# Weight blocks in another pool, X's updates with precedence, 1/rms transposed one product later

## The chip, the cores and the metric

The kernel runs on one core of one Trainium2 chip. The metric is the device time of one execution in microseconds (us), the median of several runs. A core has a matrix engine (TensorE, PE in the profile, with its weight loads as PEld), a vector engine (VectorE, DVE), an activation engine (ScalarE, ACT), a general engine (GpSimd, POOL) and SyncE (SP), which here only issues DMAs. Each works through its own instructions in order and waits on semaphores for the others. Work memory is SBUF (128 partitions); matmuls write to eight PSUM banks.

## What is computed

Two layers of a transformer with 512 tokens and width 1024 in float32: each layer is a half-step SwiGLU ffn, a mixer, and another half-step ffn, and every part is preceded by an RMS norm.

```python
def swiglu(h, w_in, w_out):
    a, b = jnp.split(h @ w_in, 2, axis=-1)
    return (jax.nn.silu(a) * b) @ w_out

for layer in range(DEPTH):                                             # 2
    g = norm_g[layer]
    x = x + 0.5 * swiglu(rmsnorm(x, g[0]), ffn_w_in[layer, 0], ffn_w_out[layer, 0])
    h = rmsnorm(x, g[1])
    x = x + (even_mixer(h, ...) if layer % 2 == 0 else odd_mixer(h, ...))
    x = x + 0.5 * swiglu(rmsnorm(x, g[2]), ffn_w_in[layer, 1], ffn_w_out[layer, 1])
return rmsnorm(x, final_norm_g)
```

The mixers are attention blocks (a gated linear attention beside a forgetting attention in the even one, an attention over the 256 best keys in the odd one). Of them only the end matters here: the output projection that is added to x.

## The kernel before

**Stages.** The program is one straight line of six stages and an end: ffn0, even, ffn1, ffn2, odd, ffn3, fin. x is kept transposed in SBUF as `X`, eight blocks of 128 features by 512 tokens.

**Precision.** Matmuls run on float32r operands. Each operand is split into a high part (`whi`, `th`, `hh`: a ScalarE copy) and a low part (`wlo`, `tl`, `hl`: a VectorE difference), and a product is three matmuls: high by high, high by low, low by high. `whi` and `wlo` have three buffers each.

**An ffn.** The 2816 hidden units are 11 pairs of 2 x 128. For each pair the first matrix product is done with seven block products instead of eight (Strassen-like). `Products` holds a pair's weight blocks `a11`, `a21` (in a `wraw` tile), `a22` and `a12`, and forms sums of them (`ws`) on VectorE in `side` (L131); `make` (L153) splits each into `whi` (L159, ScalarE) and `wlo` (L160, VectorE). The order of the products is p1, p5, p2, p6, p3, p7, p4, with p4 of a pair after p1 of the next. Each is 24 matmuls (L345). They use `th` and `tl`, combinations of the blocks of x, made by `combined` (L215) for each block as soon as X's block is final. For the first pair of an ffn `opening` (L347) runs p1, p5 and p2 first with three of the four block pairs of x (18 matmuls each) and then with the last one (6 each). The down products (eight blocks d of X, three groups of pairs; `mm3`, L195) follow in `sums` and `end` (L462 to L474): `down_end` scales the sum into `dn` (L428) and adds it to X (L429). In the last group `after(d)` then prepares the next stage's operands and the squares for the next norm.

**The norm.** The sum of squares becomes 1/rms for each token as a column, `Rc` (`rstd_cols`, L287; the rsqrt's last step is L276). `rstd_rows` (L303) transposes it to a row on all partitions with four matmuls (L307), and `rstd_tile` copies that to `R`. In pair 0 of every ffn `run` does this behind p3, and multiplies the first half of the pair's outputs by R and takes the SiLU; the later pairs use the same R.

**A mixer's end.** `out_units` (L533) loads `even_out` or `odd_out` in four `wraw` tiles, splits them (L84 and L88) and runs eight output products of 24 matmuls. `end(d)` adds the product to X (L548) and calls `after(d)`, which makes the next ffn's `th` and `tl` and adds the squares up on GpSimd (L259).

**Memory.** Pools are stacks from two ends of SBUF. From the left: small things, `wraw`, `wsp` (`whi` and `wlo`), and then, in a mixer, `mo` (operands, among them those of the output products), `mx` and `at` (scratch of attention); in an ffn `wx` (two `a22`, `a12` and `ws`, 4 KB each), `hp` and `ft`. From the right: `xp`. In an ffn it holds `th` and `tl` (four tiles of 7 KB each) and scratch of 8 KB; in a mixer `XGH` and `XGL`, eight tiles of 2 KB each. `open_in` (L1215) replaces `xp` shortly before the last output products, at which point a mixer has released `at` and `mx`. `xp` is opened with `reuse_waits="tile"`. `mo` is released only after the mixer's last instruction, and `wx` of the next ffn is allocated behind that.

**Order.** TensorE's instructions run in program order (`manual_schedule`). All others are put in order by a planner: it simulates the program and gives each engine, whenever it is free, the instruction with the lowest rank among those whose inputs are ready by its own clock; the rank is the place in the program. On the chip each engine then keeps to that order. SyncE's loads are in one queue in the same way.

Of the kernel before, what the change touches and what calls it, by code (L numbers as in the profile page):

```python
# [8 lines left out]
F32 = mybir.dt.float32  # L9
F32R = mybir.dt.float32r  # L10
U32 = mybir.dt.uint32
AF = mybir.ActivationFunctionType
# [3 lines left out]
S = 512  # L16
# [9 lines left out]
B11, T1, B21, B22, T2, T4, T3 = range(7)  # L26
# [72 lines left out]
class Products:  # L99
# [10 lines left out]
    def place(self, p, early):  # L110

        b = self.b
        w = self.blocks.setdefault(p, {})
        if early:
            raw = b.wraw.tile([128, 2048], F32, name="wraw")
            w["a11"], w["a21"] = raw[:, :1024], raw[:, 1024:]
            w["a22"] = b.wx.tile([128, 1024], F32, name="a22", bufs=2)
        else:
            w["a12"] = b.wx.tile([128, 1024], F32, name="a12", bufs=1)

    def fetch(self, p, n):
        c = ("a11", "a21", "a12", "a22").index(n) * 1024
# [8 lines left out]
    def side(self, p, q):  # L131

        w, v = self.blocks[p], self.b.nc.vector
        if q == "p1":
            return w["a11"]
        if q == "p2":
            return w["a12"]
        if q == "p4":
            return w["a22"]
        if q == "p5":  # L140
            w["s"] = self.b.wx.tile([128, 1024], F32, name="ws", bufs=1)
            v.tensor_add(w["s"], w["a21"], w["a22"])
            return w["s"]
        if q == "p6":
            v.tensor_sub(w["s"], w["s"], w["a11"])
            return w["s"]
        if q == "p3":
            v.tensor_sub(w["a12"], w["a12"], w["s"])
            return w["a12"]
        v.tensor_sub(w["a21"], w["a11"], w["a21"])  # L150
        return w["a21"]
# [12 lines left out]
class Builder:  # L164
# [160 lines left out]
    def ffn(self, n, after, first=None, lead=None):  # L325
# [5 lines left out]
        nc = self.nc  # L331
# [28 lines left out]
        def copy(name, bank, bufs):  # L360
            t = self.ft.tile([128, 2, HT], F32, name=name, bufs=bufs)
            nc.scalar.activation(t, bank.rearrange("p (f t) -> p f t", f=2), AF.Copy)
            return t

        def run(p, q, R):

            v = nc.vector
            three = lambda b: b.rearrange("p (f t) -> p f t", f=2)
            if q == "p1":
                if p:  # L370
                    d = st[p] = {"a": self.bank("ps")}
                    product(p, q, d["a"], B11, True)
                d = st[p]
                d["c1"] = copy("c1", d["a"], 1)
                return
            d = st[p]
            if q == "p5":
                if p:
                    d["b"] = self.bank("pt")
                    product(p, q, d["b"], T1, True)  # L380
                d["c5"] = copy("c5", d["b"], 1)
            elif q == "p2":
                if p:
                    d["c"] = self.bank("s")
                    product(p, q, d["c"], B21, True)
                d["t"] = self.ft.tile([128, 2, 2, HT], F32, name="ta", bufs=2)
                v.tensor_add(d["t"][:, :, 0], d["c1"], three(d["c"]))
            elif q == "p6":
                product(p, q, d["a"], T2, False)
                d["c2"] = copy("c2", d["a"], 1)  # L390
            elif q == "p3":
                product(p, q, d["b"], B22, False)
                if p == 0:
                    Rt.append(self.rstd_tile(d["rc"], "s"))
                v.tensor_add(d["t"][:, :, 1], d["c2"], three(d["b"]))
                t = d["t"].rearrange("p f h t -> p f (h t)")
                v.tensor_mul(t, t, R()[:, None, :].to_broadcast([128, 2, S]))
                self.table = "silu"
                nc.scalar.activation(t, t, AF.Silu)
            elif q == "p7":  # L400
                product(p, q, d["a"], T3, False)
                v.tensor_add(d["c5"], d["c5"], three(d["a"]))
            else:
                product(p, q, d["a"], T4, False)
                t = d["t"]
                v.tensor_mul(t[:, :, 1], t[:, :, 1], d["c5"])
                v.tensor_mul(t[:, :, 0], t[:, :, 0], three(d["a"]))
                h = [self.hp.tile([128, 2, S], F32R, name=x) for x in ("hh", "hl")]
                t = t.rearrange("p f h t -> p f (h t)")
                nc.scalar.activation(h[0], t, AF.Copy)  # L410
                v.tensor_sub(h[1], t, h[0].bitcast(F32))
                H[p] = h
                del st[p]
# [19 lines left out]
        R = lambda: Rt[0]  # L433
# [18 lines left out]
        for g, (a, b) in enumerate(GROUPS):  # L452
            last = b == NP
            seq = []
            for p in range(a + 1 if g else a, min(b + 1, NP)):
                ps = [(p, q) for q in Products.ORDER[:6]]
                if p:
                    ps.insert(1, (p - 1, "p4"))
                seq += ps
            round_(a, seq + [(NP - 1, "p4")] * last)  # L460
            banks = {}

            def begin(d):
                w = down_w(g, d)
                w.split(0)
                banks[d] = w, self.bank(tags[d % 5])

            def sums(d, pairs):
                down_mm(g, d, *banks[d], pairs)

            def end(d):
                down_end(d, banks.pop(d)[1], R())
                if last:
                    after(d)  # L474

            begin(0)
            begin(1)
            if last:
                self.next_in()
                self.lnexp()  # L480
                sums(0, range(a, b - 1))
                run(NP - 1, "p4", R)
                sums(1, range(a, b - 1))
                for d in range(2):
                    sums(d, [b - 1])
                    end(d)
                begin(2)
            for d in range(2 if last else 0, KT):
                if d + 1 < KT and d + 1 not in banks:
                    begin(d + 1)  # L490
                sums(d, range(a, b))
                if d == KT - 2:
                    W.load(b + 1, True)
                end(d)
# [38 lines left out]
    def out_units(self, src, O, after):  # L533

        nc = self.nc
        W, P = {}, {}
# [8 lines left out]
            P[d] = self.bank(tag)  # L545

        def end(d):
            nc.vector.tensor_add(self.X[:, d], P[d], self.X[:, d])  # L548
            after(d)

        early = 3
        for d in range(early):
# [633 lines left out]
    def build(self):  # L1186
        from contextlib import ExitStack
        with ExitStack() as ctx:
# [66 lines left out]
            self.squares = {}  # L1255
            start = prep(gi[st[0]], kind(0), kind(0) == "ffn")
            if kind(0) == "ffn":
                self.wx = tc.alloc_tile_pool(name="wx", bufs=1)
                first = Products(self, self.i["ffn_in"][int(st[0][3])])
                first.place(0, True)  # L1260
                first.place(0, False)
# [10 lines left out]
            for j, x in enumerate(st):  # L1272
                after = prep(gi[st[j + 1]], kind(j + 1)) if j + 1 < len(st) else last if "fin" in self.stages else lambda i: None
                self.next_in = lambda k=kind(j + 1): open_in(k)
                if x[:3] == "ffn":
                    if j:
                        self.wx = tc.alloc_tile_pool(name="wx", bufs=1)
                    with tc.tile_pool(name="hp", bufs=5) as self.hp, tc.tile_pool(name="ft", bufs=2) as self.ft:
                        self.ffn(int(x[3]), after, *((first, start) if j == 0 else ()))
                    self.wx.release()  # L1280
                    continue
                self.n_wide = 8 if x == "even" else 9
                self.next_in = lambda k=kind(j + 1): scratch_done(k)
# [102 lines left out]
```

## Time and profile before

| | us |
|---|---|
| median of three runs | 1947.22 (1940.64 to 1950.42) |
| the profiled execution | 1954.63 |
| its span, first to last instruction | 1952.8 |
| TensorE busy | 1877.9 (96%) |
| VectorE busy | 1466.5 (75%) |
| ScalarE busy | 907.8 (46%) |
| GpSimd busy | 218.1 (11%) |

The stages follow each other in the span: ffn0 to about 370 us, even to 638, ffn1 to 986, ffn2 to 1335, odd to 1590, ffn3 and the end to 1953. Matmuls overlap: a matmul of 128 x 256 has a duration of 0.28 us in the profile, but 24 of them follow each other in 2.80 us. Time on an engine that is not the limit costs nothing by itself; what counts is what TensorE waits for.

### The profile page before, as it was taken

The page shows a single profiled execution, that of the slowest core. Times are in us where ns is not written, and L with a number is a line of the kernel's source. Part 1 is how long each engine was busy: PE and PEld are TensorE (multiplying, and loading weights), DVE is VectorE, ACT ScalarE, POOL GpSimd, SP SyncE. Part 2 cuts the span into 40 slices and gives each one's busy share as a digit, 9 for nine tenths or more (in the row PEclk, how much of TensorE's full clock was granted, in tenths as well). Part 3 has the DMA queues.
Part 4 walks back from the last instruction along what each step waited for, and adds up shares of the span by engine and source line. Part 5 has one row for each costly group of instructions (what it writes and reads, how often), then busy time and mean ns, then how long its engine had stood idle before and what let it go on. Part 6 is the DMA issues. An engine that isn't in the chain of part 4 may idle for free.

```text
span 1952.8 us, 30763 instructions
## 1 busy us (share of the span) xinstructions
PE 1877.9 (96%) x12504; PEld 1687.2 (86%) x12504; DVE 1466.5 (75%) x1929; ACT 907.8 (46%) x1275; POOL 218.1 (11%) x211
## 2 busy tenths in 40 slices
PE   6999999999999899999989999999989989999997
PEld 6989999787877899989889998987766779899996
DVE  6879777557466887959798795864898589797774
ACT  5535435334354553525555352543527555354353
POOL 0000000200162000000010000011248320000001
PEclk9999999999899999999999999999999999999998
DMA  4233332322341233242423324234156123433322
GB/s 143 93 115 98 109 108 65 105 84 91 93 131 65 92 101 120 82 126 76 134 72 106 112 86 130 76 94 140 62 152 177 39 97 106 121 98 108 106 68 76
DMA packets 60510, 198.17 MB, mean 101 GB/s; under 512 B 7880, under 2 KB 8056, under 8 KB 57296
## 3 DMA queue, kind: packets, MB, share of 16 engines
q1 hardware_dynamic: 57712, 191.65, 32.1%
q10 hardware_dynamic: 2304, 4.20, 0.8%
q8 instruction: 98, 1.61, 0.3%
q0 software_dynamic: 352, 0.36, 0.1%
q14 instruction: 44, 0.36, 0.1%
HBM read 178.03 MB, written 2.15 MB: 92 GB/s over the span
## 4 chain that ended last, share of the span: by engine, by line
PE 83%; DVE 12%; issue 2%; ACT 2%; DMA 1%; POOL 0%; SPq 0%; DVEq 0%; ACTq 0%; POOLq 0%
PE ps L345 25%; PE pt L345 12%; PE s L345 6%; PE s L200 6%; PE s L198 6%; PE s L199 6%; PE ps L198 3%; PE ps L199 3%; PE ps L200 3%; DVE tl L223 2%; PE s L652 1%; DVE acc L1139 1%; PE o L686 1%; DVE wlo L88 1%; PE pt L198 1%
## 5 line engine op out<-in xcount | busy, mean ns | idle before, releaser
L345 PE MATMUL ps<-th,whi 128*128 128x256 f32 x1408 | 395.6, 281 | 9.6 <-ACT whi L159 9.6
L345 PE MATMUL ps<-th,wlo 128*128 128x256 f32 x1408 | 394.2, 280 | 0.9 <-DVE wlo L160 0.9
L345 PE MATMUL ps<-tl,whi 128*128 128x256 f32 x1408 | 394.2, 280 | 0.0
L84 ACT ACTIVATE whi<-wraw 128x1024 fp32r<-128x1024 f32 (+3 forms) x156 | 157.3, 1010 | 352.7 <-PE s L199 135.6
L345 PEld LDWEIGHTS ps<-th,whi 128*128 128x128 f32 x1408 | 266.3, 189 | 10.2 <-ACT whi L159 9.6
L345 PEld LDWEIGHTS ps<-th,wlo 128*128 128x128 f32 x1408 | 266.2, 189 | 1.4 <-DVE wlo L160 1.4
L345 PEld LDWEIGHTS ps<-tl,whi 128*128 128x128 f32 x1408 | 266.3, 189 | 0.6
L345 PE MATMUL pt<-th,whi 128*128 128x256 f32 x704 | 199.3, 283 | 17.5 <-ACT whi L159 17.5
L159 ACT ACTIVATE whi<-a 128x1024 fp32r<-128x1024 f32 x132 | 140.2, 1062 | 143.8 <-issue 45.7
L200 PE MATMUL s<-hh,wlo 128*128 128x512 f32 x528 | 205.9, 390 | 0.0
L198 PE MATMUL s<-hh,whi 128*128 128x512 f32 x528 | 205.6, 389 | 0.0
L199 PE MATMUL s<-hl,whi 128*128 128x512 f32 x528 | 205.6, 389 | 0.0
L345 PE MATMUL pt<-th,wlo 128*128 128x256 f32 x704 | 199.0, 283 | 3.1 <-DVE wlo L160 3.1
L88 DVE TENSOR_TENSOR wlo<-wraw,whi 128x1024 fp32r<-128x1024 f32 (+3 forms) x144 | 168.3, 1169 | 42.9 <-ACT whi L84 42.4
L345 PE MATMUL pt<-tl,whi 128*128 128x256 f32 x704 | 198.6, 282 | 0.0
L259 POOL TENSOR_TENSOR ss<-ss,sq 128x512 f32<-128x512 f32 x41 | 65.0, 1585 | 1155.3 <-ACT sq L255 1155.2
L160 DVE TENSOR_TENSOR wlo<-a,whi 128x1024 fp32r<-128x1024 f32 x132 | 160.9, 1219 | 9.7 <-ACT whi L159 9.7
L159 ACT ACTIVATE whi<-wraw 128x1024 fp32r<-128x1024 f32 x88 | 93.4, 1062 | 133.0 <-PE ps L345 51.6
L345 PEld LDWEIGHTS pt<-th,whi 128*128 128x128 f32 x704 | 134.8, 191 | 18.2 <-ACT whi L159 18.2
L428 DVE SCALAR_TENSOR_TENSOR dn<-s,R 128x512 f32<-128x512 f32 x72 | 49.6, 689 | 122.8 <-PE s L200 122.8
L159 ACT ACTIVATE whi<-ws 128x1024 fp32r<-128x1024 f32 x88 | 92.9, 1056 | 100.8 <-PE ps L345 62.6
L345 PEld LDWEIGHTS pt<-th,wlo 128*128 128x128 f32 x704 | 134.6, 191 | 4.2 <-DVE wlo L160 4.2
(291 smaller groups left out, 4333.8 us busy)
## 6 DMA issues: line engine op xcount, KB each, us to landing
wraw<-in_ffn_in_dram SPq DMA_DIRECT2D x88, 512.0 KB, 4.7
a<-in_ffn_in_dram SPq DMA_DIRECT2D x88, 512.0 KB, 3.8
wraw<-in_ffn_out_dram SPq DMA_DIRECT2D x64, 512.0 KB, 3.5
wraw<-in_ffn_out_dram SPq DMA_DIRECT2D x32, 384.0 KB, 3.1
x<-x SPq DMA_DIRECT2D x62, 128.0 KB, 2.3
wraw<-in_even_fox_dram SPq DMA_DIRECT2D x4, 1024.0 KB, 4.8
wraw<-in_even_out_dram SPq DMA_DIRECT2D x4, 1024.0 KB, 5.9
wraw<-in_odd_q_dram SPq DMA_DIRECT2D x8, 512.0 KB, 3.2
```

What stands on the lines that cost most here:

```text
L84: nc.scalar.activation(hi, x, AF.Copy)
L88: nc.vector.tensor_sub(lo, x, hi.bitcast(F32))
L159: b.nc.scalar.activation(o[0], x, AF.Copy)
L160: b.nc.vector.tensor_sub(o[1], x, o[0].bitcast(F32))
L198: mm(ps, w[0], x[0], start=first, stop=False)
L199: mm(ps, w[0], x[1], start=False, stop=False)
L200: mm(ps, w[1], x[0], start=False, stop=last)
L223: v.tensor_sub(l, src, h.bitcast(F32))
L259: nc.gpsimd.tensor_tensor(self.ss, self.ss, sq, op=OP.add)
L345: mm(o, w[:, c], x, start=fresh and f == j == i == 0, stop=j == 3 and i == 2, skip_group_check=True)
L428: nc.vector.scalar_tensor_tensor(t, bank, 0.5, R, op0=OP.mult, op1=OP.mult)
L652: nc.tensor.matmul(s[:, :n], q[hh][:, b * 128:b * 128 + 128], k[hh][:, :n], start=k is kh, stop=k is kl)
```

## The change

Four edits. The pool `wx` is gone: `a22`, `a12` and `ws` are now tiles of `xp`, which grows from 64 to 80 KB in an ffn, while `hp` and `ft` move 16 KB down. The X addition of `out_units` with its `after(d)` is put under `high_priority(offset=60)`, which lowers its rank by 60 places. The same holds for `down_end` and `after(d)` in an ffn's last group. And in pair 0 of an ffn the transposes of 1/rms, the copy to R, the product with R and the SiLU come behind p7 instead of p3; for the other pairs they stay behind p3.

```diff
@@ class Products
-            w["a22"] = b.wx.tile([128, 1024], F32, name="a22", bufs=2)
+            w["a22"] = b.xp.tile([128, 1024], F32, name="a22", bufs=2)
         else:
-            w["a12"] = b.wx.tile([128, 1024], F32, name="a12", bufs=1)
+            w["a12"] = b.xp.tile([128, 1024], F32, name="a12", bufs=1)
...
-            w["s"] = self.b.wx.tile([128, 1024], F32, name="ws", bufs=1)
+            w["s"] = self.b.xp.tile([128, 1024], F32, name="ws", bufs=1)
@@ def ffn
+        def gate(t, R):
+            t = t.rearrange("p f h t -> p f (h t)")
+            nc.vector.tensor_mul(t, t, R[:, None, :].to_broadcast([128, 2, S]))
+            self.table = "silu"
+            nc.scalar.activation(t, t, AF.Silu)
...
             elif q == "p3":
                 product(p, q, d["b"], B22, False)
+                v.tensor_add(d["t"][:, :, 1], d["c2"], three(d["b"]))
+                if p:
+                    gate(d["t"], R())
+            elif q == "p7":
+                product(p, q, d["a"], T3, False)
                 if p == 0:
                     Rt.append(self.rstd_tile(d["rc"], "s"))
-                v.tensor_add(d["t"][:, :, 1], d["c2"], three(d["b"]))
-                t = d["t"].rearrange("p f h t -> p f (h t)")
-                v.tensor_mul(t, t, R()[:, None, :].to_broadcast([128, 2, S]))
-                self.table = "silu"
-                nc.scalar.activation(t, t, AF.Silu)
-            elif q == "p7":
-                product(p, q, d["a"], T3, False)
+                    gate(d["t"], R())
                 v.tensor_add(d["c5"], d["c5"], three(d["a"]))
...
             def end(d):
-                down_end(d, banks.pop(d)[1], R())
                 if last:
-                    after(d)
+                    with self.tc.high_priority(offset=60):
+                        down_end(d, banks.pop(d)[1], R())
+                        after(d)
+                else:
+                    down_end(d, banks.pop(d)[1], R())
@@ def out_units
         def end(d):
-            nc.vector.tensor_add(self.X[:, d], P[d], self.X[:, d])
-            after(d)
+            with self.tc.high_priority(offset=60):
+                nc.vector.tensor_add(self.X[:, d], P[d], self.X[:, d])
+                after(d)
@@ def build
-                self.wx = tc.alloc_tile_pool(name="wx", bufs=1)
...
-                    if j:
-                        self.wx = tc.alloc_tile_pool(name="wx", bufs=1)
...
-                    self.wx.release()
```

## Rows read from the trace of the kernel before

**Rows 1.** The page: busy time by engine (part 1), the chain that ended last (part 4).

```profile
PE 1877.9 (96%) x12504; PEld 1687.2 (86%) x12504; DVE 1466.5 (75%) x1929; ACT 907.8 (46%) x1275; POOL 218.1 (11%) x211
...
PE 83%; DVE 12%; issue 2%; ACT 2%; DMA 1%; POOL 0%; SPq 0%; DVEq 0%; ACTq 0%; POOLq 0%
```

**Rows 2.** TensorE's waits, whole span: waiter, what released it, us in total, times, longest.

```profile
PE pt L345 <- ACT whi L159: 17.5, 3, 6.2
...
PE s L307 <- DVE Rc L276: 5.5, 4, 2.4
...
PE ps L200 <- DVE wlo L88: 1.6, 2, 0.8
```

**Rows 3.** TensorE in time at two hand-overs: start, us, instruction, [idle before, releaser].

```profile
637.54 0.39 PE L200 MATMUL ps<-x,wlo 128*128 128x512 f32 x1
...
646.25 0.58 PE L345 MATMUL pt<-th,whi 128*128 128x256 f32 x1 [6.21 <-ACT whi L159]
...
648.25 0.58 PE L345 MATMUL pt<-th,wlo 128*128 128x256 f32 x1 [1.20 <-DVE wlo L160]
...
1598.33 0.58 PE L345 MATMUL pt<-th,whi 128*128 128x256 f32 x1 [6.19 <-ACT whi L159]
```

**Rows 4.** VectorE and GpSimd in time at even to ffn1.

```profile
633.59 0.41 DVE L237 TENSOR_TENSOR to<-to 128x256 f32<-128x256 f32 x1
...
639.67 0.68 DVE L548 TENSOR_TENSOR X<-ps,X 128x512 f32<-128x512 f32 x1
...
641.77 1.26 POOL L259 TENSOR_TENSOR ss<-ss,sq 128x512 f32<-128x512 f32 x1 [2.57 <-ACT sq L255]
641.82 1.50 DVE L237 TENSOR_TENSOR to<-to 128x256 f32<-128x256 f32 x1
...
643.84 1.21 DVE L142 TENSOR_TENSOR ws<-wraw,a 128x1024 f32<-128x1024 f32 x1
```

**Rows 5.** SyncE's DMA issues in time (start, time until the last issue, count).

```profile
618.46 8.21 SPq L123 DMA_DIRECT2D wraw<-in_ffn_in_dram  x4
...
637.96 21.13 SPq L123 DMA_DIRECT2D a<-in_ffn_in_dram  x4
...
935.98 1.29 SPq L123 DMA_DIRECT2D a<-in_ffn_in_dram  x3
```

**Rows 6.** Stretches: PE, PEld, DVE, ACT, POOL busy (instructions), clock, DMA; last, L345 alone.

```profile
608.30:637.90 29.60, 28.82 (x128) 23.51 (x127) 26.96 (x35) 19.77 (x30) 9.02 (x6) 1.00 0.32 107
...
644.50:651.30 6.80, 3.85 (x16) 3.56 (x17) 6.77 (x7) 2.00 (x2) 0.00 (x0) 0.50 0.00 0
...
954.00:1003.00 49.00, 45.07 (x248) 38.95 (x248) 46.98 (x61) 28.16 (x43) 11.83 (x7) 1.00 0.26 77
...
50.60:54.00 3.40, 3.20 (x15) 3.27 (x16) 0.50 0.56 175
```

**Rows 7.** The chain in time: one product of 24 matmuls at the full clock.

```profile
155.73 2.80 PE s L345 x24
```

**Rows 8.** TensorE and VectorE in time at ffn1 to ffn2.

```profile
985.56 0.39 PE L200 MATMUL s<-hh,wlo 128*128 128x512 f32 x1
...
988.56 0.38 PE L345 MATMUL pt<-th,wlo 128*128 128x256 f32 x1 [0.27 <-DVE wlo L160]
...
988.76 1.21 DVE L145 TENSOR_TENSOR ws<-ws,wraw 128x1024 f32<-128x1024 f32 x1
...
991.61 0.68 DVE L428 SCALAR_TENSOR_TENSOR dn<-s,R 128x512 f32<-128x512 f32 x1
...
994.20 0.39 PE L345 MATMUL s<-th,wlo 128*128 128x256 f32 x1 [3.18 <-DVE wlo L160]
```

**Rows 9.** Uses of `XGL`: ns min/median/max, first and last start (even's stretch; whole span).

```profile
L199 PE MATMUL ps<-xgl,whi x120: 388/396/628, 374.8 to 563.9; 128*128 128x512 f32 x112, 128*48 128x512 f32 x8
...
L652 PE MATMUL s<-xgl,xgh x48: 273/375/504, 1479.9 to 1538.8; 128*128 128x128 f32 x12, 128*128 128x256 f32 x12, 128*128 128x384 f32 x12, 128*128 128x512 f32 x12
```

**Rows 10.** TensorE in time: the transposes of 1/rms in ffn1.

```profile
663.62 0.65 PE L307 MATMUL s<-ident,Rc 128*128 128x128 f32 x4 [1.06 <-DVE Rc L276]
```

## Prediction

> **What bounds the kernel now.** I read the page first. TensorE is busy 96% of the span, and the chain that ended last is 83% TensorE and 12% VectorE [rows 1]. No other engine can be the limit of the whole, so a change that adds and removes no matmul, as this one, can only win the time in which TensorE stands still or runs at its lower clock. The second view is therefore the list of what TensorE waited for. Of the lines that the diff touches it names a ScalarE split (L159) ahead of products into `pt`, 17.5 us in three waits, and the transposes of 1/rms (L307), 5.5 us in four [rows 2]. The third view is TensorE's order of time where one stage hands over to the next: there the waits sit.
>
> At the hand-over even to ffn1 the last output product issues its last matmul at 637.54, the first product's 18 matmuls follow without a gap, and then TensorE stands 6.21 us until 646.25 and 1.20 us until 648.25, for the high and the low part of the second product's weights [rows 3]. Followed back: that high part is a split of the sum `ws`, which VectorE began at 643.84 [rows 4]. The sum reads `a22`, and SyncE issued its load at 637.96, right behind the last output product, though `a11` and `a21` had gone out from 618.46 on [rows 5]. The load waits because `wx` lies where the mixer's `mo` lay, and `mo` holds the operand of that very product. odd to ffn3 repeats all this; its longer wait is 6.19 us [rows 3]. The pause is followed by TensorE's lower clock level: 0.50 of the full clock (1.2 for 2.4 GHz) from 644.5 to 651.3 [rows 6], and likewise in ffn3.
>
> ffn1 to ffn2 is different: its loads went out at 935.98 [rows 5], fifty us before the last down product ended, yet TensorE waits 0.27 and 3.18 us [rows 8]. The cause is VectorE, busy 46.98 of the 49 us around it [rows 6]: `dn` of the last product runs at 991.61, 5.7 us after that product's last matmul (985.56 + 0.39), behind work of the next ffn such as the difference at 988.76 (L145) [rows 8].
>
> **The change part by part.** *The blocks in `xp`.* The loads no longer wait for `mo`. By tile sizes an ffn's `xp` is now 80 KB at the top of SBUF against the mixer's 32 KB, so the 16 KB of blocks lie over `XGL` if tiles are laid in the order of their first use, else over `at` or `mx`. `XGL` was last read at 563.9 in even and at 1538.8 in odd [rows 9]; `at` and `mx` fall out of use when attention ends, before the output products that bound the hand-over. On SyncE's queue the loads stand at the latest behind the four of `a11` and `a21`, so they go out by 618.46 + 8.21 = 626.7 [rows 5]. Today's load of 637.96 was read at 643.84, under 6 us later, so they land by 633. Behind them in that queue stand only pair 1's loads.
>
> What is late next? The second product's split needs one of three `whi` buffers, free when the seventh output product ends, 24 matmuls or some 5.5 us before 637.9; add about 1.1 us on ScalarE and 1.2 on VectorE, as the sum takes (1.21) [rows 4], and it is there before 640. The third product's split needs the buffer of the last output product: 637.9 + 1.1 + 1.2 = 640.2, against a need at 637.8 + 2 x 2.1 = 642 (18 matmuls at 2.80/24 us each [rows 7]). That is 1.8 us of slack if VectorE is on time. Today the last X addition starts 1.7 us late, at 639.67 [rows 4], and now a sum, two differences and a split, 4 x 1.2 us, may come ahead of it; VectorE had 29.60 - 26.96 = 2.6 us idle before 637.9 to take them [rows 6]. So X would be some 4 us late and the third split, right behind it, 1 to 2 us. I leave 1.0 us of wait at each hand-over, between 0 and the 3.18 + 0.27 = 3.45 us of ffn1 to ffn2; nearer the low end, because here no `dn` (0.7 us for each block) burdens VectorE.
>
> Won at each: 6.21 + 1.20 us of standing, plus the clock: 16 matmuls took 3.85 us busy from 644.5 to 651.3 [rows 6], at the full rate 16 x 2.80/24 = 1.87, so 2.0 us. Sum 9.4, less 1.0 is 8.4. **Two hand-overs: -16.8 us** (bounds -11.9 and -18.8).
>
> *1/rms a product later.* TensorE waits 1.06 us at the transposes of ffn1 for the end of the rsqrt [rows 10], at most 2.4 us (in ffn0), 5.5 in all four [rows 2]. With p7 ahead of the transposes TensorE has 2.80 us more work first [rows 7], more than each wait, so all go: 5.5 us. In ffn0 half clock stands behind that gap, 15 matmuls in the 3.40 us from 50.6 on [rows 6]; at the full rate they take 1.75, and the four transposes 0.65 [rows 10], so 1.0 us more. What else moves: the copy of R, a table load, the product with R and the SiLU, on ScalarE and VectorE, now beside pair 1's first product; the addition to `c5` stands behind them in the program, and pair 0's fourth product overwrites the bank that it reads, 2.80 us after the transposes. Copy, product and addition are 0.7 + 1.2 + 0.7 = 2.6 us (as an X addition and the sum `ws`, which have those sizes [rows 4]), hidden by pair 1's p1; with one split of 1.2 in front they cost 1.0 us, four times. **-6.5 us** (bounds -2.5 and -6.5). I take the full gain, since the addition's inputs are there before the product's are, and it can go first.
>
> *Precedence.* It rewinds the rank of X's update and its combinations by 60 instructions, about two products. At ffn1 to ffn2 it can win up to 3.45 us, if VectorE takes `dn` earlier. But `dn` already stands ahead of the next ffn's work in the program and is overtaken by it in the trace [rows 8], so the planner took it to be not ready yet, and rank doesn't help what isn't ready. I take **-1.0** (bounds 0 and -3.45). Where rank does act is against the splits of later output weights (L88). These are late twice, 1.6 us in all [rows 2], and could be earlier or twice as late: **0** (bounds -1.6 and +1.6).
>
> Here a rule may speak against the change. Row first: one and the same VectorE difference took 0.41 us at 633.59 and 1.50 at 641.82, when GpSimd's addition of squares had begun at 641.77 [rows 4]. The Trainium skill, GPSIMD Engine Reference, section Specifications, says that GpSimd shares its SBUF interfaces with VectorE and contends with instructions of two SBUF inputs. The trace agrees, with 1.1 us a meeting. By that rule an earlier X update only moves the meeting, in the worst case onto the third product's split, and the sum would be 2 x 1.1 us smaller.
>
> **Sum.** -16.8 - 6.5 - 1.0 = -24.3 us on the profiled execution of 1954.6 us (span 1952.8 and 1.8 around it), which is 1930.3. That execution is 7.4 us above the median of 1947.2; the same difference gives **1922.9 us**. Bounds: all good -18.8 - 6.5 - 3.45 - 1.6 = -30.4, 1917; all bad -11.9 - 2.5 + 1.6 = -12.8, 1934.
>
> **The rivals.** *VectorE takes the DMA's place.* Each mixer hand-over comes out as ffn1 to ffn2 does today, with 3.45 us of waits, and nothing is won there: -11.9 - 6.5 = -18.4, 1928.8 us. For: VectorE is busy 26.96 of 29.60 us before the hand-over [rows 6]. Against: what of that comes late is mostly not the split that TensorE needs first.
> *The loads don't go out early*, held by SyncE's queue or by a tile below them that is read late. Then only 1/rms and the 1.0 are won: 1939.7 us, no difference that counts. For: SyncE's queue is in order, and one load in front that waits holds all behind it. Against: the tiles below are read for the last time, and the loads in front are out, by 627 [rows 5, 9].
> *Slower: a weight split behind X's chain.* With X ahead in rank, `dn` and X (0.7 us each) come in front of the split for the next output product; VectorE waits for the running product, and TensorE for VectorE. There are 48 output products (six stages of eight). It decides from 24.3 / 48 = 0.5 us of wait per product on; at 1.4 each it is 67.2 - 24.3, 1990 us. For: X's rank now lies two products earlier. Against: today such a split is late twice in the whole span [rows 2], and its inputs are ready earlier than the running product's end.
>
> **How the numbers follow.** Forecast 0.63 (its own range 1917 to 1934), VectorE 0.23, loads not early 0.08, slower 0.06. A measurement of this kernel tells about 0.5%, 9.7 us, from no change, so faster means below 1937.5: forecast and the VectorE case but for a sliver, 0.85; same, the loads and that sliver, 0.10; slower 0.05. The range that holds 8 in 10 runs from 1912 (all good, less some 0.25%, by which the runs shown lie off their median) to 1936 (all bad, plus 2).
>
> **What would show it.** Right: `a22`'s load in SyncE's order before the last output product ends; no TensorE wait over 2 us in the first products of ffn1 and ffn3, and no half clock behind them; no wait at the transposes but the one at the kernel's end. Wrong: waits for L160 of 3 to 4 us there (VectorE), loads still behind the last output product, new waits for L88 within output products, or a wait of the fourth product for `c5`.

## The result, and the profile after

The changed kernel takes 1923.92 us (median of four runs, 1921.11 to 1928.37) where the kernel before, run beside it, took 1948.82: a ratio of 0.9878, with a 95% interval from 0.9837 to 0.9919. A second series gave 0.9876 (0.9849 to 0.9903). That is 24 us (the intervals: 16 to 32 us and 19 to 29 us); the forecast was 1922.9 us, 24.3 us less than 1947.2. The profiled execution took 1925.84 us, its span is 1924.0.

The page, in the same parts as [rows 1]: TensorE's busy time is 11 us less than before, though no matmul is added or taken away; the rest of the span's 28.8 us is time in which it stood.

```profile
PE 1866.9 (97%) x12504; PEld 1677.3 (87%) x12504; DVE 1467.4 (76%) x1929; ACT 907.5 (47%) x1275; POOL 217.8 (11%) x211
...
PE 84%; DVE 12%; ACT 1%; DMA 1%; issue 1%; SPq 0%; DVEq 0%; ACTq 0%
```

TensorE's waits over the whole span (us in total, times, longest), to be held against [rows 2]. The wait for L159 ahead of `pt` was 17.5 us in three and is now one, at the kernel's start. The transposes of 1/rms (L307) wait only at the kernel's end. But output products wait for L88 four times instead of twice.

```profile
PE pt L345 <- ACT whi L159: 5.1, 1, 5.1
PE s L345 <- DVE wlo L160: 4.8, 4, 3.2
...
PE ps L200 <- DVE wlo L88: 3.0, 4, 0.8
...
PE ps L307 <- DVE Rc L276: 1.8, 1, 1.8
```

TensorE in time at even to ffn1, at the transposes in ffn1, at ffn1 to ffn2 and at odd to ffn3 ([rows 3, 8, 10] of before). After the last output product (628.04) the first two products run through, and the third waits 0.59 us for its low part; the transposes wait for nothing. At ffn1 to ffn2 the 3.17 us are what they were.

```profile
628.04 0.39 PE L200 MATMUL ps<-x,wlo 128*128 128x512 f32 x1
...
633.46 0.39 PE L345 MATMUL s<-th,wlo 128*128 128x256 f32 x1 [0.59 <-DVE wlo L160]
...
647.58 0.60 PE L307 MATMUL s<-ident,Rc 128*128 128x128 f32 x4
...
975.28 0.58 PE L345 MATMUL s<-th,wlo 128*128 128x256 f32 x1 [3.17 <-DVE wlo L160]
...
1575.65 0.38 PE L345 MATMUL s<-th,wlo 128*128 128x256 f32 x1 [0.60 <-DVE wlo L160]
...
1581.50 0.38 PE L345 MATMUL ps<-th,wlo 128*128 128x256 f32 x1 [0.33 <-DVE wlo L160]
```

SyncE's issues ([rows 5]): the loads of `a22` and `a12` go out 64 us (even) and 52 us (odd) ahead of the last output products' ends.

```profile
564.48 1.37 SPq L123 DMA_DIRECT2D a<-in_ffn_in_dram  x3
...
1518.89 1.28 SPq L123 DMA_DIRECT2D a<-in_ffn_in_dram  x3
```

What held them until then is seen in odd, in the uses of `XGL` (first and last start): its last matmul starts at 1518.4, and at 1518.89 the first load goes out. In even they stand behind another DMA of the queue, until 564.48.

```profile
L661 PE MATMUL s<-xgl,xgh x48: 273/375/504, 1458.5 to 1518.4; 128*128 128x128 f32 x12, 128*128 128x256 f32 x12, 128*128 128x384 f32 x12, 128*128 128x512 f32 x12
```

Stretches of 6.8 us (PE, PEld, DVE, ACT, POOL busy, then the granted clock), behind even's hand-over and behind ffn1's. Where [rows 6] had 16 matmuls at 0.50 there are 51 at the full clock. The second stretch is new in this execution: behind the 3.17 us wait the clock falls to 0.50 (1.2 GHz), which it did not do behind the 3.18 us of before (last section).

```profile
633.40:640.20 6.80, 6.41 (x51) 6.13 (x52) 6.77 (x10) 4.72 (x8) 1.54 (x1) 1.00 0.01 2
974.30:981.10 6.80, 5.82 (x27) 5.82 (x28) 5.63 (x7) 3.37 (x5) 1.53 (x1) 0.50 0.00 0
```

VectorE at even to ffn1 ([rows 4]). The last X addition starts at 631.59, 3.2 us after the last output product's last matmul has ended (628.04 + 0.39), because a weight sum (L145) and a difference that met GpSimd (1.78 us) lie ahead of it; the split that TensorE waits for is right behind it.

```profile
628.75 1.22 DVE L145 TENSOR_TENSOR ws<-ws,wraw 128x1024 f32<-128x1024 f32 x1
629.88 1.78 DVE L223 TENSOR_TENSOR tl<-te,th 128x512 fp32r<-128x512 f32 x1
631.59 0.68 DVE L557 TENSOR_TENSOR X<-ps,X 128x512 f32<-128x512 f32 x1
632.19 1.21 DVE L160 TENSOR_TENSOR wlo<-a,whi 128x1024 fp32r<-128x1024 f32 x1
```

### The profile page after: what moved, and what is told of

Read it like the earlier page. It is cut to its first block, busy times and chain, and to the rows that moved or that the text cites. A ratio compares the mean times of both kernels' runs of the same rounds, so it can differ in the third digit from the quotient of the medians.

```text
span 1924.0 us, 30748 instructions
## 1 busy us (share of the span) xinstructions
PE 1866.9 (97%) x12504; PEld 1677.3 (87%) x12504; DVE 1467.4 (76%) x1929; ACT 907.5 (47%) x1275; POOL 217.8 (11%) x211
## 4 chain that ended last, share of the span: by engine, by line
PE 84%; DVE 12%; ACT 1%; DMA 1%; issue 1%; SPq 0%; DVEq 0%; ACTq 0%
PE ps L345 25%; PE pt L345 12%; PE s L200 6%; PE s L345 6%; PE s L198 6%; PE s L199 6%; PE ps L198 3%; PE ps L199 3%; PE ps L200 3%; DVE tl L223 2%; PE s L661 2%; DVE acc L1148 1%; DVE wlo L88 1%; PE o L695 1%; PE pt L680 1%
## 5 line engine op out<-in xcount | busy, mean ns | idle before, releaser
L345 PE MATMUL ps<-th,whi 128*128 128x256 f32 x1408 | 394.8, 280 | 10.0 <-ACT whi L159 10.0
L345 PE MATMUL ps<-th,wlo 128*128 128x256 f32 x1408 | 394.1, 280 | 1.1 <-DVE wlo L160 1.1
L345 PE MATMUL ps<-tl,whi 128*128 128x256 f32 x1408 | 393.4, 279 | 0.0
L345 PEld LDWEIGHTS ps<-th,whi 128*128 128x128 f32 x1408 | 265.5, 189 | 10.7 <-ACT whi L159 10.0
L345 PEld LDWEIGHTS ps<-th,wlo 128*128 128x128 f32 x1408 | 265.5, 189 | 1.8 <-DVE wlo L160 1.8
L345 PEld LDWEIGHTS ps<-tl,whi 128*128 128x128 f32 x1408 | 265.6, 189 | 0.6
L159 ACT ACTIVATE whi<-a 128x1024 fp32r<-128x1024 f32 x132 | 140.0, 1061 | 144.3 <-PE pt L345 43.9
L200 PE MATMUL s<-hh,wlo 128*128 128x512 f32 x528 | 205.9, 390 | 0.0
L345 PE MATMUL pt<-th,whi 128*128 128x256 f32 x704 | 197.4, 280 | 5.1 <-ACT whi L159 5.1
L88 DVE TENSOR_TENSOR wlo<-wraw,whi 128x1024 fp32r<-128x1024 f32 (+3 forms) x144 | 168.6, 1172 | 39.5 <-ACT whi L84 39.2
L345 PE MATMUL pt<-th,wlo 128*128 128x256 f32 x704 | 197.4, 280 | 0.7 <-DVE wlo L160 0.7
L345 PE MATMUL pt<-tl,whi 128*128 128x256 f32 x704 | 197.0, 280 | 0.0
L159 ACT ACTIVATE whi<-wraw 128x1024 fp32r<-128x1024 f32 x88 | 93.4, 1062 | 131.7 <-PE ps L345 51.7
L345 PEld LDWEIGHTS pt<-th,whi 128*128 128x128 f32 x704 | 133.2, 189 | 5.4 <-ACT whi L159 5.4
L345 PEld LDWEIGHTS pt<-th,wlo 128*128 128x128 f32 x704 | 133.0, 189 | 1.2 <-DVE wlo L160 1.2
L345 PEld LDWEIGHTS pt<-tl,whi 128*128 128x128 f32 x704 | 133.2, 189 | 0.0
```

The costliest lines, as they stand in the source:

```text
L88: nc.vector.tensor_sub(lo, x, hi.bitcast(F32))
L159: b.nc.scalar.activation(o[0], x, AF.Copy)
L200: mm(ps, w[1], x[0], start=False, stop=last)
L345: mm(o, w[:, c], x, start=fresh and f == j == i == 0, stop=j == 3 and i == 2, skip_group_check=True)
```

## The experiments

Ratios are against the kernel before, run on the same chip in the same series, with 95% intervals.

### The parts alone

**Only the blocks in `xp`** (with `wx` gone, and no other edit of the change):

```diff
-            w["a22"] = b.wx.tile([128, 1024], F32, name="a22", bufs=2)
+            w["a22"] = b.xp.tile([128, 1024], F32, name="a22", bufs=2)
...
-            w["a12"] = b.wx.tile([128, 1024], F32, name="a12", bufs=1)
+            w["a12"] = b.xp.tile([128, 1024], F32, name="a12", bufs=1)
...
-            w["s"] = self.b.wx.tile([128, 1024], F32, name="ws", bufs=1)
+            w["s"] = self.b.xp.tile([128, 1024], F32, name="ws", bufs=1)
```

> Only the blocks of weights go into xp; 1/rms and the ranks stay as before. My theory (the loads of a22 and a12 are what TensorE waited for, and precedence does nothing at the hand-overs): the loads go out some 70 us earlier, the first products of ffn1 and ffn3 wait 1 us in all instead of 7.4, and the span gets 16 to 17 us shorter than the kernel before; the waits of the 1/rms transposes (L307, 5.5 us in four) stay, the three waits of output products for L88 splits stay at 1.6 us in two. Rival (VectorE takes the DMA's place unless X's updates have precedence): waits for L160 of 3 us and more at both hand-overs, and 11 to 12 us won.

Measured: 0.9917 (0.9895 to 0.9939), which is 16.2 us of 1949.46. TensorE at even to ffn1, and its clock over the seven microseconds:

```profile
638.88 0.39 PE L345 MATMUL s<-th,wlo 128*128 128x256 f32 x1 [1.23 <-DVE wlo L160]
...
644.72 0.38 PE L345 MATMUL ps<-th,wlo 128*128 128x256 f32 x1 [0.33 <-DVE wlo L160]
```

```profile
638.00:645.00 7.00, 5.79 (x46) 5.51 (x47) 6.97 (x9) 4.92 (x8) 1.53 (x1) 1.00 0.01 2
```

The hand-over is won without precedence. The waits left are 1.56 us, where I had expected 1.0. The L307 and L88 waits are those of before (5.4 us in four, 1.6 in two). The rival falls.

**Only 1/rms behind p7:**

```diff
             elif q == "p3":
...
+                if p:
+                    gate(d["t"], R())
             elif q == "p7":
                 product(p, q, d["a"], T3, False)
                 if p == 0:
                     Rt.append(self.rstd_tile(d["rc"], "s"))
+                    gate(d["t"], R())
```

> Only the transposes of 1/rms and the gate of pair 0 go behind p7. My theory: the L307 waits but the end's go, with the half clock behind that of ffn0, and the span gets 5 to 6.5 us shorter than the kernel before; the waits of 6.2 and 1.2 us at the two mixer hand-overs stay. Rival (the copy, the product with R, the SiLU and the addition to c5, now beside pair 1's first product, hold up TensorE there): up to 1 us is given back in each ffn, 2.5 us won.

Measured: 0.9963 (0.9944 to 0.9982), 7.2 us. The hand-over waits are those of before, and of L307 only the end's is left; no product waits for the bank that the addition to `c5` frees.

```profile
PE pt L345 <- ACT whi L159: 17.5, 3, 6.2
...
PE ps L307 <- DVE Rc L276: 1.8, 1, 1.8
```

**Only the precedence:**

```diff
-            nc.vector.tensor_add(self.X[:, d], P[d], self.X[:, d])
-            after(d)
+            with self.tc.high_priority(offset=60):
+                nc.vector.tensor_add(self.X[:, d], P[d], self.X[:, d])
+                after(d)
```

(and likewise around `down_end` and `after` in an ffn's last group)

> Only the precedence for X's update and its combinations. My theory (VectorE's order at ffn1 to ffn2 doesn't change, and in the mixers an L88 split moves behind two differences): nothing won, 0 to 1.5 us lost, in one or two more waits of 0.75 us of an output product for L88; the 3.2 us wait at ffn1 to ffn2 stays. Rival (precedence brings X forward): that wait falls to under 1.5 us, and 1 to 3.5 us are won.

Measured: 1.0022 (1.0004 to 1.0040), slower if anything. The waits for L88 double, and the hand-over waits lose 0.45 us each (6.2 to 5.76 and 5.74):

```profile
PE pt L345 <- ACT whi L159: 16.5, 3, 5.8
...
PE ps L200 <- DVE wlo L88: 3.1, 4, 0.8
PE s L345 <- DVE wlo L160: 2.9, 2, 2.4
```

The wait at ffn1 to ffn2 is 2.44 us here. That is no gain of precedence: the kernel before with `wx` opened in another way (below), with VectorE's order of before, has 2.45 there too, and the changed kernel has had 3.17 in one execution and 2.43 in another. What differs is a meeting. GpSimd's addition of squares starts 0.02 us behind a VectorE sum of 1.21 us (L145); after that sum either GpSimd's addition goes next and VectorE's difference takes 1.77 us, or the difference goes next and takes 0.68. The changed kernel in its two executions:

```profile
971.00 1.77 DVE L223 TENSOR_TENSOR tl<-te,th 128x512 fp32r<-128x512 f32 x1
```

```profile
975.73 0.68 DVE L223 TENSOR_TENSOR tl<-te,th 128x512 fp32r<-128x512 f32 x1
```

In the second, the X addition that follows takes 1.05 us instead of 0.69, so that 0.73 us is left of the 1.09: the difference of the two waits. Of the eight traces in which VectorE's instructions stand in this order there, four have the one (3.17 to 3.19 us) and four the other (2.43 to 2.45). The rows for L88 and the hand-overs account for 0.6 us lost (1.5 - 0.9) of the 0.8 to 7.8 that the interval spans; what else there is, if anything, stays open.

**The changed kernel without precedence, beside the changed kernel:** the two `with self.tc.high_priority(offset=60):` are replaced by `if True:`.

> The changed kernel as it is, beside the three variants of it that follow: about 1924 us, 0.988 of the kernel before.

> The changed kernel without the precedence. Its instructions stand as in the changed kernel on every engine but VectorE and ScalarE, and there only after the first three output products of either mixer, where a split for a later output product (L88) stands ahead of two differences again. My theory: the second L88 wait of 0.72 to 0.76 us in each mixer goes; the rest stays, but VectorE's differences move by one split, so the wait at the hand-over may come back to the 1.23 us that blocks alone left, from 0.59. Sum between -1.5 and 0 us against the changed kernel. Rival (precedence is worth microseconds, as its place in the change suggests): waits for L160 of 3 us and more at the mixer hand-overs, 5 us slower.

Measured: 0.9876 (0.9849 to 0.9903) with precedence and 0.9874 (0.9849 to 0.9900) without: the same. The traces show two shifts that nearly cancel. With precedence, TensorE's wait at even to ffn1 and its waits for L88:

```profile
638.20 0.39 PE L345 MATMUL s<-th,wlo 128*128 128x256 f32 x1 [0.64 <-DVE wlo L160]
```

```profile
PE ps L200 <- DVE wlo L88: 3.1, 4, 0.8
```

Without it:

```profile
641.10 0.38 PE L345 MATMUL s<-th,wlo 128*128 128x256 f32 x1 [1.27 <-DVE wlo L160]
```

```profile
PE ps L200 <- DVE wlo L88: 1.6, 2, 0.8
```

In each mixer precedence puts five VectorE instructions (two differences and three combinations) ahead of one split for a later output product; on VectorE only these six change places. TensorE then waits some 0.75 us for that split, and some 27 us further on it waits 0.63 us less for the last low split. At ffn1 to ffn2 VectorE's instructions stand in the same order with and without it, and the waits are the same (0.27 and 2.43 against 0.27 and 2.44).

### Place, or kind of wait?

The kernel before, with `wx` opened as `xp` is:

```diff
-                self.wx = tc.alloc_tile_pool(name="wx", bufs=1)
+                self.wx = tc.alloc_tile_pool(name="wx", bufs=1, reuse_waits="tile")
```

(in both places)

> The kernel before, with wx opened in the way in which xp is (a tile waits for the tiles that lay in its place, not for all of the released pool). If the place is what holds the loads (a22 lies over an operand of the last output product), they still go out behind that product and nothing changes, within 2 us. If it is the kind of wait, they go out up to 70 us earlier and 16 us are won without moving any tile to xp.

Measured: 1.0016 (0.9993 to 1.0039), nothing won. The loads go out 0.9 us ahead of the start of the last output product's last matmul (in the kernel before 0.4 behind it, [rows 3, 5]), and TensorE waits as before. SyncE, then TensorE:

```profile
636.79 1.28 SPq L123 DMA_DIRECT2D a<-in_ffn_in_dram  x3
```

```profile
637.73 0.39 PE L200 MATMUL ps<-x,wlo 128*128 128x512 f32 x1
...
646.44 0.58 PE L345 MATMUL pt<-th,whi 128*128 128x256 f32 x1 [6.22 <-ACT whi L159]
```

So it is the place: SyncE's wait ahead of these loads still ends with a matmul of an output product (L200), so that what `a22` lies over is read until shortly before the last one's end. And the 1.4 us by which the loads are earlier come to nothing, since VectorE's order is that of before: the sum `ws` stands behind the differences of the last X and starts at 644.03, though `a22` landed at 640.76. In the kernel before it is the same, with `a22` there at 642.08 and the sum at 643.84: the last 1.8 us of that wait are VectorE's order, not the load. With the blocks in `xp` the sum stands far ahead of the last X in VectorE's order (at 614.04 in the changed kernel), so that the move wins both parts together; no run parts them.

### What is left at the hand-overs

**The sums queued behind X.** On top of the change, the sums of p6, p3 and p7 of an ffn's first pair come behind p2's low split on VectorE (`low2` is that instruction):

```diff
-        x = self.side(p, q)
+        with b.tc.issue_after(self.low2) if p == 0 and q in ("p6", "p3", "p7") else nullcontext(): x = self.side(p, q)
```

> The changed kernel, with one thing more: for the first pair of each ffn the weight sums of p6, p3 and p7 on VectorE (L145, L148, L150) are queued behind the low split of p2 (L160), and so behind dn and X's last update. If it is VectorE's order that makes TensorE wait 3.2 us at ffn1 to ffn2 (three sums of 1.2 us in front of the last dn), that wait falls under 1.5 us, and the half clock behind it goes; at the mixer hand-overs the 0.6 us goes too: 2 to 5 us won against the changed kernel. Rival (VectorE's work as a whole binds there, 47 of 49 us busy): the wait only moves to the later products, as waits for L160 of p6, p3 or p7, and nothing is won or 1 to 2 us are lost.

Measured: 0.9910 (0.9883 to 0.9937), 6.5 us slower by the medians than the changed kernel in the same series (1934.25 and 1927.72 us). The two intervals still touch, but the traces agree: ffn1, ffn2 and ffn3 take 2.3, 3.1 and 1.6 us more from their first L345 matmul to the last. My theory falls, and the rival holds with more than its price of 1 to 2 us. TensorE at even to ffn1 and at ffn1 to ffn2:

```profile
645.06 0.38 PE L345 MATMUL ps<-th,wlo 128*128 128x256 f32 x1 [2.08 <-DVE wlo L160]
...
981.38 0.39 PE L345 MATMUL s<-th,wlo 128*128 128x256 f32 x1 [1.67 <-DVE wlo L160]
...
985.83 0.39 PE L345 MATMUL s<-tl,whi 128*128 128x256 f32 x1 [0.78 <-DVE tl L223]
...
990.10 0.43 PE L345 MATMUL ps<-th,wlo 128*128 128x256 f32 x1 [2.06 <-DVE wlo L160]
```

The third product's wait is gone at the mixers and shorter at ffn1 to ffn2, but the fourth (p6) waits 2.1 us at each, and behind it the clock falls (0.66 from 990 to 995 us). VectorE's work comes due product by product: what is put behind one split makes the next late.

**The same without precedence** (the two `with` lines as `if True:` again):

> e5's order without the precedence. If both theories hold it has the L88 waits of 1.6 us in two and no wait over 1.5 us at any hand-over: 3 to 6 us under the changed kernel. If precedence matters once the sums are out of VectorE's way, it is slower than the variant with precedence.

Measured: 0.9931 (0.9908 to 0.9955), which is 10.9 us slower by the medians than the changed kernel and clear of its interval; I had expected 3 to 6 us less. The same waits of 2.0 to 2.1 us for p6. Between this and the one above the intervals overlap, so that what precedence does there isn't told apart.

**One sum on GpSimd.** On top of the change, p6's sum of the first pair in ffn1, ffn2 and ffn3 (`self.n` counts the ffns from 1):

```diff
-            v.tensor_sub(w["s"], w["s"], w["a11"])
+            (v if p or self.n == 1 else self.b.nc.gpsimd).tensor_tensor(w["s"], w["s"], w["a11"], op=OP.subtract)
```

> The changed kernel with three VectorE instructions on GpSimd: the sum of p6 (L145, 1.2 us) for the first pair of ffn1, ffn2 and ffn3. Nothing else stands in another order. If VectorE's work as a whole binds at the hand-overs, as the variant with the sums queued behind X made likely, the wait for the last low split shrinks by the 1.2 us: 0.64 to 0 at the two mixers, 2.7 to about 1.5 at ffn1 to ffn2, and the half clock behind the latter may go as well: 2 to 5 us under the changed kernel. Rival (VectorE's instructions beside GpSimd's get longer by as much, 0.41 to 1.5 us for a difference beside the addition of squares in the kernel before): the differences and splits beside L145 take 1 us more each, the waits stay as they are or grow, 0 to 3 us lost.

Measured: 0.9869 (0.9834 to 0.9905), no different from the changed kernel. GpSimd, VectorE and TensorE at even to ffn1:

```profile
628.47 2.85 POOL L145 TENSOR_TENSOR ws<-ws,wraw 128x1024 f32<-128x1024 f32 x1
631.28 2.27 POOL L259 TENSOR_TENSOR ss<-ss,sq 128x512 f32<-128x512 f32 x1
```

```profile
629.58 2.82 DVE L160 TENSOR_TENSOR wlo<-a,whi 128x1024 fp32r<-128x1024 f32 x1
632.33 1.50 DVE L236 TENSOR_TENSOR to<-to,te 128x256 f32<-128x256 f32 x1
```

```profile
632.46 0.39 PE L345 MATMUL s<-th,wlo 128*128 128x256 f32 x1 [1.20 <-DVE wlo L160]
```

VectorE is rid of 1.2 us, and p2's split, which meets that sum, takes 2.82 us instead of 1.21. TensorE's wait is 1.20 us instead of 0.6, and 3.50 at ffn1 to ffn2. The rival holds.

**The same without precedence:**

> The same without the precedence. If the relief is real, the hand-over wait of 1.27 us that the variant without precedence left falls to 0.1, and the second L88 wait of 0.75 us in each mixer is not there: 1.5 us better than with precedence. If it isn't, 1.3 us and more remain at each mixer and the two are alike.

Measured: 0.9874 (0.9840 to 0.9907). Waits of 1.86 us at both mixers and of 3.50 at ffn1 to ffn2, and 1.6 us for L88: alike, as the rival has it.

**Only p7's sum put off**, behind p6's low split, in ffn1 to ffn3:

```diff
-        x = self.side(p, q)
+        with b.tc.issue_after(self.low6) if (p, q) == (0, "p7") and self.n > 1 else nullcontext(): x = self.side(p, q)
```

> The changed kernel, with the weight sum of p7 (L150, 1.2 us of VectorE) of the first pair in ffn1, ffn2 and ffn3 queued behind the low split of p6. It is the one sum that VectorE does before the hand-overs and that no product needs until the sixth. If VectorE's work before the last low split sets the hand-over waits, and a sum put off this far comes out of it without being missed later, the wait at ffn1 to ffn2 falls by 1.2 us (2.4 to 3.5 at present), those at the mixers from 0.6 to 0, and 2 to 5 us are won. Rival (as with the sums of p6, p3 and p7 together): the work only moves behind, and p6, p3 or p7 wait instead, with nothing won or up to 3 us lost.

Measured: 0.9872 (0.9847 to 0.9898). At the mixers the 0.6 us is gone and the 0.33 stays. TensorE at ffn1 to ffn2:

```profile
979.21 0.39 PE L345 MATMUL s<-th,whi 128*128 128x256 f32 x1 [0.31 <-ACT whi L159]
...
981.15 0.39 PE L345 MATMUL s<-th,wlo 128*128 128x256 f32 x1 [1.43 <-DVE wlo L160]
...
985.59 0.39 PE L345 MATMUL s<-tl,whi 128*128 128x256 f32 x1 [0.78 <-DVE tl L223]
...
988.07 0.39 PE L345 MATMUL ps<-th,wlo 128*128 128x256 f32 x1 [0.27 <-DVE wlo L160]
```

One wait of 2.4 to 3.2 us, with one of 0.25 ahead of it, has become four of 2.79 in all, and the clock stays at 1.00 behind them, from 970 to 995 us. Both theories are half right: at the mixers the wait goes, at ffn1 to ffn2 it is spread. What that wins is not more than the runs can tell.

**The same in ffn2 alone** (`self.n == 3`):

> The same in ffn2 alone, where VectorE is fullest: 1.2 us off the 2.4 to 3.5 us wait at ffn1 to ffn2, and perhaps its half clock, 1 to 3 us won and nothing changed at the mixers; the rival has it move to p6, p3 or p7 of ffn2.

Measured: 0.9886 (0.9862 to 0.9910); the same four waits at ffn1 to ffn2, the mixers as in the changed kernel. None of these versions is faster than the changed kernel by more than the intervals, and the two with all three sums queued are slower by the medians.

## Why the prediction was right

| term | forecast (bounds) | measured |
|---|---|---|
| blocks in `xp` | -16.8 (-11.9 and -18.8) | alone -16.2 (-11.9 to -20.5) |
| 1/rms behind p7 | -6.5 (-2.5 and -6.5) | alone -7.2 (-3.5 to -10.9) |
| precedence, ffn1 to ffn2 | -1.0 (0 and -3.45) | 0: same order, same wait |
| precedence, L88 | 0 (-1.6 and +1.6) | +1.5 in the waits, set off by -1.3 at the hand-overs |
| sum | -24.3 | -23.8 and -24.2 |

Measured in us: the ratio's distance from 1, times the median of before in that series. The two parts alone make 23.4 us, so they add up as far as the intervals tell, and precedence is not needed for either: without it 24.6 us are won.

**The bound.** TensorE's waits and the half clock behind them were the right place to look. In the two profiled executions ffn1 and ffn3 each take 9.4 us less from their first L345 matmul to the last (308.4 and 308.5 to 299.1), ffn0 has lost its 2.37 us wait and 1.0 us of half clock, and ffn2 its 1.0 us wait for 1/rms: 23.2 us, where the two large terms have 23.3. Against it stand some 1.5 us for L88 and the new half clock in ffn2.

The size of the sum is borne out less well than it looks. The measured intervals are 16 and 10 us wide, so that 24 us against 24.3 is in part luck; and the 1.0 us for precedence, which did not come, lies far within them.

**The hand-overs.** Each step held. The loads went out when `XGL` was read for the last time (odd), or some 10 us later, when the DMA in front of them in SyncE's queue had gone out (even). My bound of 626.7 was 62 us later than what came; how late they could go out wasn't tried. What was late next was what the prediction named: the high and low parts of the second product were there, and the third product's low split was 1.23 us late behind the last X, for which I had said 1 to 2. The 1.0 us that I left was 1.56 with the blocks alone and 0.92 in the changed kernel. The half clock behind the old waits is gone from both hand-overs, as the sum had it.

**1/rms.** All four waits went, and the half clock of ffn0 with them. (That 1.0 us was not sure: with the blocks alone the same wait, 2.36 us, has no half clock behind it.) The cover, one product of 2.80 us, was longer than the longest wait of 2.37. The addition to `c5` cost nothing, as taken.

**Precedence** is where my number was wrong, though its reason was right. I had written that rank doesn't help what isn't ready and then still took 1.0 us; VectorE's order at ffn1 to ffn2 is the same, and the term is 0. On L88 it ended close to the unfavourable bound, with the waits doubled (1.6 to 3.0 us), where I had taken 0. I had not seen that the same exchange halves the wait at the hand-over; the two nearly cancel.

**The rivals.** *VectorE takes the DMA's place*: not as priced (3.45 us at each hand-over, against 0.92). But the last experiments show that it is VectorE which sets what is left: sums put off come back as waits of p6, a sum sent to GpSimd as a longer split. *The loads don't go out early* fell with the first row of SyncE. *Slower, a weight split behind X's chain*: the mechanism is there, with the sign named for it (new waits for L88), but at 0.75 us and in two more of 48 products instead of in all.

**The rule that spoke against the change** (meetings of VectorE with GpSimd) was worth its place, though its price was too simple. At even to ffn1 a meeting now falls on the difference just ahead of the last X (1.78 us, where one without a meeting takes 0.68). That is 1.1 us in front of the third product's split, and the wait for that split is 0.59: by these rows (an estimate) there would be none without the meeting. I had 1.1 us for a meeting. In the rows of VectorE and GpSimd under *One sum on GpSimd* the split ends 1.08 us after GpSimd's sum (628.47 + 2.85 = 631.32; 629.58 + 2.82 = 632.40), not much less than the 1.21 that it takes by itself, and the addition that GpSimd starts at 631.28 ends 1.15 us after that split. Each takes nearly its whole time once the other is done: the price is what is left of the other's instruction. The Trainium skill, SBUF — State Buffer, section SBUF: two separate sides, has it so: whichever starts first holds the shared ports for its whole instruction. The trace agrees, with 1.6 us for this meeting.

**The profiled executions** differ by more than the runs, 28.8 us against 24. Of that 4 us is TensorE's pace at the kernel's start, which differs from execution to execution (last section). Up to 5 us more (an estimate from 10.2 us at half the pace) is the lower clock level in even and odd, ahead of their output products, where the change touches nothing: it was granted there for 27.3 us in before, 17.1 in after, and 27.3 in the other execution of the changed kernel. Three stretches of before, then of after (second figure: TensorE busy, with the number of matmuls):

```profile
25.00:30.00 5.00, 5.00 (x25) 5.00 (x25) 2.43 (x3) 1.96 (x3) 0.00 (x0) 1.00 0.00 0
30.00:35.00 5.00, 5.00 (x25) 5.00 (x25) 0.91 (x2) 2.39 (x4) 0.00 (x0) 1.00 0.01 3
35.00:40.00 5.00, 5.00 (x37) 5.00 (x37) 1.41 (x4) 2.48 (x4) 0.00 (x0) 1.00 0.00 0
```

```profile
25.00:30.00 5.00, 5.00 (x30) 5.00 (x30) 2.43 (x3) 1.98 (x3) 0.00 (x0) 1.00 0.00 0
30.00:35.00 5.00, 5.00 (x45) 5.00 (x45) 1.03 (x2) 3.48 (x7) 0.00 (x0) 1.00 0.02 3
35.00:40.00 5.00, 5.00 (x46) 5.00 (x45) 4.76 (x7) 5.00 (x8) 0.00 (x0) 1.00 0.00 0
```

Before has 34 matmuls fewer in these 15 us, 4.0 us at 2.80 for 24. The forecast was made as a difference and carried to the median, and so these chances did not enter it.

## What to carry to other kernels

When a load goes out late, ask which tile lies where it is to land, and who reads that tile last: another place for the blocks won 16 us here, where another kind of wait in the same place won nothing. Precedence changes only the order of what the planner holds to be ready at the same time, and what it brings forward puts something else back; read the order before you give it a number. Where an engine's work comes due piece by piece, a piece put off comes back as the next wait, and a piece sent to an engine that it meets (GpSimd here) comes back as a longer instruction.

## What was not expected of the hardware

**At the start of the kernel the matmuls go at about half the pace for a time that differs between executions whose instructions are the same up to there.** The rows above have 25 matmuls in 5 us where 45 stand once the pace has risen. It rose at about 29 us in one execution of the changed kernel; without precedence, in the profiled execution, it was still at the low pace at 45 to 50 us, with TensorE busy all that time:

```profile
45.00:50.00 5.00, 5.00 (x25) 5.00 (x25) 2.70 (x4) 0.04 (x1) 0.00 (x0) 1.00 0.64 210
```

The clock of 1.00 in all these rows is no reading. The traces' records of the granted clock begin only at 36.9 us in before, 28.8 in after and 50.9 without precedence, and the view prints 1.00 where there is none. In all fourteen traces the pace rises within 2 us of the first record. So the lower level up to there fits (at 0.50, behind the 3.17 us wait, 27 matmuls took 5.82 us, about this pace), but no record says it, and what ends the slow time the runs do not show. It is one reason why two profiles are poor material for a difference of a few microseconds.

**The same wait has the half clock behind it or not.** Of the eight traces with a wait of 2.43 to 3.19 us at ffn1 to ffn2, six have it. Behind the 3.18 us wait of before [rows 8] the clock stayed at 1.00 (the first row below, over 986 to 996 us), as behind that of 3.18 us with the blocks alone; behind 3.17 us in the changed kernel it read 0.50 for 6.8 us, and behind 2.43 us in another execution of it 0.73 over 980 to 985 us (the second fence).

```profile
986.00:996.00 10.00, 6.54 (x53) 6.12 (x52) 9.96 (x12) 5.12 (x8) 3.88 (x2) 1.00 0.00 0
```

```profile
980.00:985.00 5.00, 5.00 (x35) 5.00 (x34) 4.26 (x5) 2.26 (x3) 1.05 (x1) 0.73 0.00 0
```

In the changed kernel's 6.8 us, 27 matmuls took 5.82 us, and at the full clock they take 27 x 2.80/24 = 3.15. So a wait of this length can cost its own length and 2.7 us more, or nothing more. What decides it the runs do not show.
